# A block's evaluation moved by one pair, the end of the last quarter in an order by hand, and roots refined in three operations

## The chip, the cores and the metric

The kernel runs on one core of a Trainium2 chip. The time is that of the device, in microseconds (us), for one execution; given are the median of several runs and their range. The core has a tensor engine (PE, with its weight loads PEld), a vector engine (DVE), an activation engine (ACT), GpSimd (POOL) and an engine that mostly issues transfers (SP). Each works through its own queue in order and waits on semaphores. Transfers between HBM and the on-chip memory (SBUF) run on 16 DMA engines. Products are accumulated in PSUM, in eight banks of 128 x 512 fp32.

## What is computed

One encoder block over a sequence of 1024 tokens of width 1024, in fp32:

```python
h = h + 0.5 * swiglu(rms_norm(h, ffn1_norm), w_gate, w_up, w_down)      # width 2816
u = rms_norm(h, mix_norm)
z = u @ w_in                     # q, k, v, state-space input, two gates
y_attn = neighbourhood_attention(q, k, v, na_rpb) @ w_attn_out
y_ssm  = s5_branch(s_in, lam, log_dt, b, c, d, glu) @ w_ssm_out   # 32 groups, 2 directions
h = h + (sigmoid(g_attn) * y_attn + sigmoid(g_ssm) * y_ssm) @ w_out
h = h + 0.5 * swiglu(rms_norm(h, ffn2_norm), w_gate2, w_up2, w_down2)
h = h + (p @ ple_w_proj) * sigmoid(rms_norm(h, ple_norm) @ ple_w_gate)
out = rms_norm(h, final_norm)
```

`rms_norm(x, g)` is `x * rsqrt(mean(x*x) + eps) * g`.

## The kernel before

**Layout.** Everything is kept transposed: channels on the 128 partitions, tokens along a row, in two halves t = 0, 1 of 512 tokens. `h[j][t]` is channel block j (of 8), half t.

**Products.** A fp32 operand is split into two parts in the format fp32r: a high part (ACT, L149) and the rest (DVE subtracts, L150). `mm3` (L180 to L182) makes a product from three matmuls of such parts. After each `mm3` the code calls `tick`, which lets one side generator go on when its count has run down: so DVE, ACT and PE work of another stage is placed between the products. `yield n` in a generator means: n ticks until its next piece.

**The feed-forward layers (class `Ffn`).** A 2 x 2 block product is made with seven products in place of eight. The 22 blocks of the hidden width form 11 pairs. Pair 0 of the first layer is special (`run_plain`): its four blocks c = 11, 12, 22, 21 are made as plain fp32 products of h times the norm's gain, without the norm's root r, and DVE multiplies the results by r afterwards (`evac_plain`, L558 to L562). For the second operand of a block (`up`) this is put off: `finish_plain` (L669) does it inside the next block, and for the last block, 21, in pair 1 (L718). There it is six DVE operations: L561, L562 and the four of `combine` (L533, L535, L537, L539), with stores to `a_d`.

Pairs 1 to 10 are items ("A", p, i, g): pair p, product i of seven, g = 0 gate or 1 up, so 14 items for each pair. For each item n the code first prepares the operand of item n + 4 (`prep`, `b_operand`: for i = 2, 3, 5, 6 a subtraction, L425 or L427, then the split), runs four `mm3` into bank Z, X or Y (`ACC7 = "ZXYXYXX"`) and evaluates the result (`evac_a`: a copy on ACT, or L580 and L586 on DVE and the SiLU on ACT). A bank X that takes i = 6 on top of i = 5 must first have been read by L580 for i = 5.

**Who sets the order.** PE's order is the order of the program text for the whole kernel. For DVE and ACT it is so only from the start until `begun`, which was called at item (2,0,0), that is p = 2, i = 0, g = 0 (L720). Afterwards a planner orders DVE, ACT, POOL and SP by a priority (earlier in the text is first, and work under `high_priority` counts as 300 instructions earlier) and by a simulated time. `begun` also closes the pool `up`, which holds r and sums of squares of the start (`acc`, `rs`, `q`), and opens the pool "g" of the state-space parameters in the same room.

**State-space parameters (`gen_all`, L983).** When "g" is there, `gen_params` computes the discretised parameters: some hundred small DVE operations over 46 ticks, ending in the powers `pw` (L818 to L856). POOL copies them to `pe` and `pg` (L867, L870: 68 copies). Then for each of 16 pairs of groups `gen_pair` makes the matrices `gm` and `em` on POOL (L903 to L924); 25 ticks later PE transposes `gm` (`tp`, L947) and multiplies `em` (`kp`, L958). Between `gen_params` and the first `gen_pair` stands `yield 10` (L990).

**Roots (`rstd`, L200).** ACT takes an approximate 1/sqrt, and DVE refines it with one Newton step in four operations (L202 to L205). It is called eleven times. The rows named `gains` hold five norms' gains for each channel; every use of a root is multiplied by one of them.

**The end.** The last layer works in parts: part 0 is half 0, part 1 and 2 are the quarters of half 1 (256 tokens each), part 3 is both quarters at once. `embed(m, part)` (L1582) makes the gate product `pg` and the embedding product `pp` of block m, then sigmoid on ACT (L1596), product and sum on DVE (L1601, L1602), the square for the final norm (`fin[i].add`, L217 to L224), and multiplies h by the final gain on ACT (L1607). `finish(part)` (L1609) takes the root and multiplies four times two blocks by it (L1617), each followed by a store (L1618). The sigmoid and the root need different ACT tables, each loaded by an ACT_TABLE_LOAD; a tiny root on `dummy` (L1600) loads the last one ahead of need. The last steps are blocks 6 and 7 of quarter 1, then of quarter 2; quarter 1 is finished while quarter 2 is made.

Of the kernel before, what the change touches and what calls it, by code (L numbers as in the profile page):

```python
# [11 lines left out]
AF = mybir.ActivationFunctionType  # L12
ALU = mybir.AluOpType
# [3 lines left out]
P = 128  # L17
# [3 lines left out]
NK = 8  # L21
# [17 lines left out]
def encoder_block(ctx, tc, I, out):  # L39
    nc = tc.nc  # L40
    V, A, G, T = nc.vector, nc.scalar, nc.gpsimd, nc.tensor

    sb = ctx.enter_context(tc.tile_pool(name="sb", bufs=1))
    ps = ctx.enter_context(tc.tile_pool(name="ps", bufs=8, space=PSUM))
    dr = ctx.enter_context(tc.tile_pool(name="dr", bufs=1, space=DRAM))

    def const(name, shape, cols=16):


        n = math.prod(shape[1:])  # L50
        t = sb.tile([shape[0], -(-n // cols) * cols], F32, name=name)[:, 0:n]
        if len(shape) == 2:
            return t
        dims = " ".join("abcd"[:len(shape) - 1])
        return t.rearrange(f"p ({dims}) -> p {dims}", **dict(zip("bcd", shape[2:])))
# [12 lines left out]
    def at(kind, shape, dt, name):  # L68
        pool, tag, bufs = cur[kind]
        return pool.tile(list(shape), dt, tag=tag, bufs=bufs, name=name)  # L70
# [10 lines left out]
    def tmp(name, shape=(P, HT), dt=F32):  # L81
        return at("tmp", shape, dt, name)
# [4 lines left out]
    def bank(name):  # L87
        return ps.tile([P, HT], F32, tag="ps", name=name)
# [4 lines left out]

    gains = const("gains", [P, 5, NK])
    nc.sync.dma_start(gains, I["gains"])
    ones = const("ones", [P, P])
    V.memset(ones, 1.0 / SEQ)
    eps = const("eps", [P, 2])
    dummy = eps[:, 1:2]
    eps = eps[:, 0:1]  # L100
# [21 lines left out]
    def start(gen):  # L122
        side["gen"], side["wait"] = gen, next(gen, None)
        if side["wait"] is None:
            side["gen"] = None
# [15 lines left out]
    def drain():  # L141
        gen, side["gen"] = side["gen"], None
        if gen is not None:
            for _ in gen:
                pass
# [6 lines left out]
    def ksl(k):  # L152
        return slice(k * P, (k + 1) * P)
# [35 lines left out]
    def new_h():  # L189
        hb = whole["hb"] = tl("h", 1, [P, 2 * XR], F32, "hbuf")  # L190
        whole["h"] = hb[:, 0:2 * NK * HT].rearrange("p (j t c) -> p j t c", t=2, c=HT)
        return [[hb[:, (2 * j + t) * HT:(2 * j + t + 1) * HT] for t in range(2)] for j in range(NK)]
# [7 lines left out]
    def rstd(m, r, q):  # L200
        A.activation(r, m, AF.Abs_reciprocal_sqrt, bias=eps)
        V.tensor_tensor(q, r, r, ALU.mult)  # L202
        V.scalar_tensor_tensor(q, m, eps, q, ALU.add, ALU.mult)
        V.tensor_scalar(q, q, -0.5, 1.5, ALU.mult, ALU.add)
        V.tensor_tensor(r, r, q, ALU.mult)  # L205

    class Norm:

# [93 lines left out]
    def after(n, fn):  # L302
        def gen():
            yield n
            fn()
        return gen()
# [128 lines left out]
    class Ffn:  # L435
# [261 lines left out]
        def run(self):  # L697
            items = [("C", c, g) for c in C4 for g in range(2)]
            items += [("A", p, i, g) for p in range(1, NP2) for i in range(7) for g in range(2)]
            items += [("B", i, j) for i in range(7) for j in range(NP2)]  # L700
            nl = np_ = 0
            for n, item in enumerate(items):
                while nl < min(len(items), n + self.lb + 1):
                    self.load(items[nl])
                    nl += 1
                while np_ < min(len(items), n + self.la + 1 if n > 7 or not self.seven.plain else 8):
                    if items[np_] not in self.made:
                        self.prep(items[np_])
                    np_ += 1
                if item[0] == "C" and self.seven.plain:  # L710
                    if item[2] == 0:
                        self.run_plain(item[1])
                    self.second = n == 7
                    continue
                if item[0] == "C":
                    self.run_c(*item[1:])
                    continue
                if item == ("A", 1, 3, 0):  # L718
                    self.finish_plain()
                if item == ("A", 2, 0, 0) and self.seven.plain:  # L720
                    self.begun()
                if item[0] == "A":
                    self.run_a(item)
                    continue
                _, i, j = item
                if item in self.hooks:
                    self.hooks[item]()
                if i < 6 or j < NP2 - 4:
                    for q in range(4):
                        self.run_b(i, j, q)  # L730
                elif j == NP2 - 1:
                    for q in range(4):
                        for jj in range(NP2 - 4, NP2):
                            self.run_b(i, jj, q)
                if i == 4 and j == NP2 - 1:
                    self.t0_done()
# [149 lines left out]
    def load_bc(pr):  # L886
        if pr < NPAIR:
            bcs[pr] = pools["g"].tile([P, 6, 2, 16], F32, tag="bc", bufs=1, name="bc")
            nc.sync.dma_start(bcs[pr], I["ssm_bc"][pr])
# [86 lines left out]
    h = new_h()  # L976
# [8 lines left out]
    def gen_all():  # L985
        while "g" not in pools:
            yield 1
        yield from gen_params()
        load_bc(0)
        yield 10  # L990
        for pr in range(NPAIR):
            fin = gen_pair(pr)
            yield 25
            fin()
            yield 4
# [386 lines left out]
    for tt in range(NK):  # L1382
        o = bank("v")
        t, c0 = tt // 4, (tt % 4) * P
# [47 lines left out]
    for hp in range(4):  # L1432
# [3 lines left out]
        n = 2 if hp < 3 else 6  # L1436
# [23 lines left out]
    h = new_h()  # L1460
# [48 lines left out]
    for m0 in range(0, NK, 2):  # L1509
        W, Wn, last = Wn, [], m0 == NK - 2  # L1510
# [34 lines left out]
    def ple_w(*ms):  # L1545
        for m in ms:
            W[m] = loadh(I["wpg"][m])
# [31 lines left out]

    fin = [Fin(i) for i in range(3)]  # L1580

    def embed(m, part):  # L1582
        t, c0, c1 = parts[part] if part < 3 else (1, 0, HT)
        n = c1 - c0
        end = part == 2 and m == NK - 1
        a, b = bank("pg")[:, 0:n], bank("pp")[:, 0:n]
        for k in range(NK):
            mm3(a, W[m][k], [x[:, c0:c1] for x in pn[t][k]], k == 0, k == NK - 1)
            tick()
        for k in range(2):  # L1590
            mm3(b, wpp[m // 4][(m % 4) * 2 + k], [x[:, c0:c1] for x in phl[k, t]], k == 0, k == 1)
            tick()
        s = tmp("ps", [P, n])
        hm = h[m][t][:, c0:c1]
        with tc.high_priority(offset=PRI):
            sg = A.activation(s, a, AF.Sigmoid)  # L1596
            if end:

                with tc.issue_after(sg.ins):
                    dm = A.activation(dummy, eps, AF.Abs_reciprocal_sqrt)  # L1600
            V.tensor_tensor(s, s, b, ALU.mult)  # L1601
            V.tensor_tensor(hm, hm, s, ALU.add)  # L1602
            for i in ((1, 2) if part == 3 else (part,)):
                with (tc.issue_after(dm.ins) if end else nullcontext()):
                    fin[i].add(m, V, end)
        if not end:
            A.activation(hm, hm, AF.Copy, scale=gains[:, 4, m:m + 1])  # L1607

    def finish(part):  # L1609
        f = fin[part]  # L1610
        t, c0, c1 = parts[part]
        f.stat()
        hv = whole["h"][:, :, t, c0:c1]
        if part == 2:
            A.activation(hv[:, NK - 1], hv[:, NK - 1], AF.Copy, scale=gains[:, 4, NK - 1:NK])
        for j in range(0, NK, 2):
            V.tensor_tensor(hv[:, j:j + 2], hv[:, j:j + 2], f.r.unsqueeze(1).broadcast_to([P, 2, f.n]), ALU.mult)  # L1617
            nc.sync.dma_start(out.rearrange("(j p) c -> p j c", p=P)[:, j:j + 2, f.osl], hv[:, j:j + 2])  # L1618

    steps = [(m, 0) for m in range(4)] + [(m, 3) for m in range(4)] + [(m, 0) for m in range(4, NK)]  # L1620
    steps += [(4, 3), (5, 3), (6, 1), (7, 1), (6, 2), (7, 2)]
    ahead = {0: (2,), 1: (3,), 3: (4,), 5: (5,), 6: (6,), 7: (7,)}
    for n, (m, part) in enumerate(steps):
        ple_w(*ahead.get(n, ()))
        if n == 0:
            for k in range(2):
                st = tmp("pst")
                nc.sync.dma_start(st, I["pT"][ksl(k), hsl(1)])
                phl[k, 1] = (tx("pph"), tx("ppl"))
                split(*phl[k, 1], st)  # L1630
            wpp.append(loadh(I["wpp"][1], w_kind="hid"))
        embed(m, part)
        if (m, part) == (3, 0):
            drain()
        if m == NK - 1 and part < 2:
            start(after((14, 9)[part], lambda part=part: finish(part)))
    drain()
    finish(2)


def _layout(x, p, ffn1_norm, ffn1_w_gate, ffn1_w_up, ffn1_w_down, mix_norm, w_in, na_rpb,
# [87 lines left out]
```

## Time and profile before

| | us |
|---|---|
| median of 3 runs | 2150.05 |
| range of the runs | 2149.36 to 2153.09 |
| the profiled execution | 2153.29 |
| its span, first to last instruction | 2151.5 |
| mean granted clock of PE in it | 0.991 |

The profiled execution is 3.2 us above the median; its span leaves out 1.8 us that lie around the instructions. In the profile's tables a row of the timeline reads: start, duration, engine, line, operation, output<-input, shapes, count, and in brackets the idle time before it and what ended it. A row of waits reads: who waited for whom, total us, number of times, the longest. A row of windows reads: the stretch, its length, the busy time of PE, PEld, DVE, ACT and POOL with instruction counts, the granted clock of PE (1 is full), the share of the DMA engines and GB/s. A row of groups reads: shape and count, busy us and mean ns, then idle time before and what ended it.

### The profile page before, as it was taken

To read this page: it belongs to the slowest core of one execution; us is meant where nothing else is said; L and a number is where in the kernel's file an instruction comes from. 1 tells how busy PE (TensorE), PEld (TensorE's weight loads), DVE (VectorE), ACT (ScalarE), POOL (GpSimd) and SP (SyncE) were. 2 spreads that over 40 slices of the span, in tenths; PEclk is the share of its full clock that TensorE was granted. 3 is DMA by queue.
4 is the path that set the end of the run, shared out by engine and by line. 5 is a ranking of instruction groups with operands and counts; after the bars stand their busy time and mean duration, and the time that the engine had idled before them with its cause. 6 is when DMAs were issued, how large, how long until landed. Compare 5 with 4: busy or idle time off the path is not lost.

```text
span 2151.5 us, 28464 instructions
## 1 busy us (share of the span) xinstructions
PE 2101.7 (98%) x9708; PEld 1721.1 (80%) x9708; DVE 1423.6 (66%) x2462; ACT 985.3 (46%) x1830; POOL 392.4 (18%) x680
## 2 busy tenths in 40 slices
PE   8999999999999999999999999899999999999997
PEld 3688888878888888888887788688888888888886
DVE  7886776666967334767744665986666565785845
ACT  6433333334445334666864422543333334545543
POOL 0047555540000008887000000000000000000000
PEclk9999999999999999999999999899999999999999
DMA  3524443466533452223576631242323338533302
GB/s 130 159 86 156 128 131 129 137 208 221 184 116 118 139 176 80 76 68 100 150 216 234 206 103 59 93 156 80 125 89 105 116 94 283 172 107 94 118 20 78
DMA packets 201105, 282.06 MB, mean 131 GB/s; under 512 B 42624, under 2 KB 85760, under 8 KB 200960
## 3 DMA queue, kind: packets, MB, share of 16 engines
q1 hardware_dynamic: 186112, 259.27, 38.1%
q10 hardware_dynamic: 14848, 20.98, 2.8%
q8 instruction: 76, 1.25, 0.2%
q14 instruction: 69, 0.57, 0.1%
HBM read 197.86 MB, written 82.31 MB: 130 GB/s over the span
## 4 chain that ended last, share of the span: by engine, by line
PE 88%; DVE 4%; DMA 4%; ACT 2%; issue 1%; SPq 0%; DVEq 0%; ACTq 0%
PE dx L180 4%; PE dx L181 4%; PE dx L182 4%; PE gx L180 3%; PE gx L182 3%; PE gx L181 3%; PE ux L180 3%; PE ux L182 3%; PE ux L181 3%; PE dy L182 2%; PE dy L181 2%; PE dy L180 2%; PE gy L180 2%; PE uy L180 2%; PE gy L181 2%; PE uy L181 2%
## 5 line engine op out<-in xcount | busy, mean ns | idle before, releaser
L149 ACT CAST wh<-hbuf 128x512 fp32r<-128x512 f32 x280 | 173.3, 622 | 411.3 <-PE gx L181 89.1
L150 DVE TENSOR_TENSOR wl<-hbuf,wh 128x512 fp32r<-128x512 f32 x280 | 208.9, 747 | 133.6 <-ACT wh L149 133.2
L149 ACT CAST wh<-wblk 128x512 fp32r<-128x512 f32 x162 | 100.6, 622 | 165.0 <-PE dx L181 68.5
L150 DVE TENSOR_TENSOR wl<-wblk,wh 128x512 fp32r<-128x512 f32 x162 | 112.4, 695 | 47.3 <-ACT wh L149 43.1
L150 DVE TENSOR_TENSOR al<-araw,ah 128x512 fp32r<-128x512 f32 x154 | 106.9, 697 | 55.0 <-PE dx L181 21.1
L180 PE MATMUL dx<-ah,wh 128*128 128x512 f32 x352 | 138.1, 392 | 0.5 <-DVE hbuf L693 0.5
L182 PE MATMUL dx<-ah,wl 128*128 128x512 f32 x352 | 137.0, 389 | 0.0
L181 PE MATMUL dx<-al,wh 128*128 128x512 f32 x352 | 137.0, 389 | 0.0
L1095 POOL TENSOR_TENSOR sc<-X,rho 128x128 f32<-128x128 f32 x128 | 71.7, 560 | 345.5 <-ACT X L1078 335.5
L180 PE MATMUL gx<-xh,wh 128*128 128x512 f32 x320 | 126.5, 395 | 7.0 <-DVE c L580 7.0
L182 PE MATMUL gx<-xh,wl 128*128 128x512 f32 x320 | 126.0, 394 | 0.0
L181 PE MATMUL gx<-xl,wh 128*128 128x512 f32 x320 | 125.6, 393 | 0.0
L180 PE MATMUL ux<-xh,wh 128*128 128x512 f32 x320 | 124.9, 390 | 0.0
L182 PE MATMUL ux<-xh,wl 128*128 128x512 f32 x320 | 124.5, 389 | 0.0
L181 PE MATMUL ux<-xl,wh 128*128 128x512 f32 x320 | 124.5, 389 | 0.0
L149 ACT CAST ah<-araw 128x512 fp32r<-128x512 f32 x154 | 94.9, 619 | 50.5 <-DVE al L150 13.9
L180 PE MATMUL gt<-xh,wh 128*128 128x512 f32 x256 | 102.9, 402 | 0.0
L182 PE MATMUL gt<-xh,wl 128*128 128x512 f32 x256 | 100.0, 391 | 0.0
L181 PE MATMUL gt<-xl,wh 128*128 128x512 f32 x256 | 99.9, 390 | 0.0
L425 DVE TENSOR_TENSOR hbuf<-hbuf 128x512 f32<-128x512 f32 x120 | 91.1, 759 | 2.4 <-DMA hbuf<-in_wg 0.4
L180 PEld LDWEIGHTS dx<-ah,wh 128*128 128x128 f32 x352 | 66.1, 188 | 15.8 <-DVE hbuf L693 1.7
L180 PEld LDWEIGHTS gx<-xh,wh 128*128 128x128 f32 x320 | 60.9, 190 | 21.1 <-issue 5.5
(375 smaller groups left out, 5769.2 us busy)
## 6 DMA issues: line engine op xcount, KB each, us to landing
araw<-a_d SPq DMA_DIRECT2D x154, 256.0 KB
a_d<-c SPq DMA_DIRECT2D x148, 256.0 KB
wblk<-in_wd SPq DMA_DIRECT2D x88, 256.0 KB
hbuf<-in_wg SPq DMA_DIRECT2D x40, 512.0 KB
hbuf<-in_wu SPq DMA_DIRECT2D x40, 512.0 KB
wst<-in_win SPq DMA_DIRECT2D x26, 512.0 KB
hbuf<-in_xT SPq DMA_DIRECT2D x32, 256.0 KB
h_d<-hbuf ACTq DMA_DIRECT2D x32, 256.0 KB
```

The source lines that it names most:

```text
L149: A.copy(hi, src)
L150: return eng.tensor_tensor(lo, src, hi.bitcast(F32), ALU.subtract)
L180: T.matmul(o, lhsT=wh, rhs=xh, start=first, stop=False, skip_group_check=more)
L181: T.matmul(o, lhsT=wh, rhs=xl, start=False, stop=False, skip_group_check=more)
L182: T.matmul(o, lhsT=wl, rhs=xh, start=False, stop=last, skip_group_check=more)
L425: V.tensor_tensor(b11, (b12, b22, None, None, b21)[i - 2], b11, ALU.subtract)
L1095: G.tensor_tensor(sc, both, rho4, ALU.mult)
```

## The change

Three edits:

1. `finish_plain` for block 21 of pair 0, and `begun` with it, are called at item (2,1,0), so in the third pair's second product. Before, `finish_plain` was called at (1,3,0) and `begun` at (2,0,0). DVE's and ACT's order by hand goes on until there. `yield 10` ahead of the first `gen_pair` becomes `yield 2`.
2. `rstd` gives -2 times the root, in three DVE operations; all `gains` are multiplied by -0.5 once at the start.
3. The end of the last two steps is written out in a function `end`, under an order by hand of DVE and ACT: quarter 1's four scalings are set one behind the sum of block 6, one behind its squares' sum, and two behind the sum of block 7.

```diff
     nc.sync.dma_start(gains, I["gains"])
+
+    V.tensor_scalar(gains, gains, -0.5, None, ALU.mult)
...
         V.tensor_tensor(q, r, r, ALU.mult)
         V.scalar_tensor_tensor(q, m, eps, q, ALU.add, ALU.mult)
-        V.tensor_scalar(q, q, -0.5, 1.5, ALU.mult, ALU.add)
-        V.tensor_tensor(r, r, q, ALU.mult)
+        V.scalar_tensor_tensor(r, q, -3.0, r, ALU.add, ALU.mult)
...
-                if item == ("A", 1, 3, 0):
+                if item == ("A", 2, 1, 0) and self.seven.plain:
                     self.finish_plain()
-                if item == ("A", 2, 0, 0) and self.seven.plain:
                     self.begun()
...
         yield from gen_params()
         load_bc(0)
-        yield 10
+        yield 2
...
+    def first_out():
+        fin[0].stat()
+        finish(0)
+
+    def end():
+
+        start(after(9, fin[1].stat))
+        six = products(6, 2)
+        drain()
+        A.activation(six[2], six[0], AF.Sigmoid)
+        added(*six)
+        finish(1, (0,))
+        fin[2].add(6)
+        scaled(6, six[3])
+        finish(1, (2,))
+        a, b, s, hm = products(7, 2)
+        A.activation(s, a, AF.Sigmoid)
+
+        A.activation(dummy, eps, AF.Abs_reciprocal_sqrt)
+        added(a, b, s, hm)
+        fin[2].add(7, last=True)
+        scaled(7, hm)
+        finish(1, (4, 6))
+        fin[2].stat()
+        finish(2)
...
-    steps += [(4, 3), (5, 3), (6, 1), (7, 1), (6, 2), (7, 2)]
+    steps += [(4, 3), (5, 3), (6, 1), (7, 1)]
...
-        if m == NK - 1 and part < 2:
-            start(after((14, 9)[part], lambda part=part: finish(part)))
+        if m == NK - 1 and part == 0:
+            start(after(14, first_out))
     drain()
-    finish(2)
+    with tc.manual_schedule(engines={mybir.EngineType.DVE, mybir.EngineType.Activation}):
+        end()
```

`products` makes the two products of a block as `embed` did, `added` is L1601 and L1602, `scaled` is L1607, and `finish(part, js)` now scales and stores only the blocks js and leaves the root to its caller.

More of the change, by code (lines that the diff above doesn't have):

```diff
@@ L1580, in encoder_block, with products @@
     fin = [Fin(i) for i in range(3)]
-    def embed(m, part):
+    def products(m, part):
         t, c0, c1 = parts[part] if part < 3 else (1, 0, HT)
         n = c1 - c0
-        end = part == 2 and m == NK - 1
         a, b = bank("pg")[:, 0:n], bank("pp")[:, 0:n]
@@ L1592, in embed @@
             tick()
-        s = tmp("ps", [P, n])
-        hm = h[m][t][:, c0:c1]
-        with tc.high_priority(offset=PRI):
[L1596 to L1602, printed above, removed]
-            for i in ((1, 2) if part == 3 else (part,)):
-                with (tc.issue_after(dm.ins) if end else nullcontext()):
-                    fin[i].add(m, V, end)
@@ L1606, in embed, with added, scaled @@
-        if not end:
-            A.activation(hm, hm, AF.Copy, scale=gains[:, 4, m:m + 1])
-    def finish(part):
+        return a, b, tmp("ps", [P, n]), h[m][t][:, c0:c1]
+    def added(a, b, s, hm):
+        V.tensor_tensor(s, s, b, ALU.mult)
+        V.tensor_tensor(hm, hm, s, ALU.add)
+    def scaled(m, hm):
+        A.activation(hm, hm, AF.Copy, scale=gains[:, 4, m:m + 1])
+    def embed(m, part):
+        a, b, s, hm = products(m, part)
+        with tc.high_priority(offset=PRI):
+            A.activation(s, a, AF.Sigmoid)
+            added(a, b, s, hm)
+            for i in ((1, 2) if part == 3 else (part,)):
+                fin[i].add(m)
+        scaled(m, hm)
@@ L1610, in finish @@
+    def finish(part, js=range(0, NK, 2)):
         f = fin[part]
         t, c0, c1 = parts[part]
-        f.stat()
         hv = whole["h"][:, :, t, c0:c1]
-        if part == 2:
-            A.activation(hv[:, NK - 1], hv[:, NK - 1], AF.Copy, scale=gains[:, 4, NK - 1:NK])
-        for j in range(0, NK, 2):
+        for j in js:
             V.tensor_tensor(hv[:, j:j + 2], hv[:, j:j + 2], f.r.unsqueeze(1).broadcast_to([P, 2, f.n]), ALU.mult)
             nc.sync.dma_start(out.rearrange("(j p) c -> p j c", p=P)[:, j:j + 2, f.osl], hv[:, j:j + 2])
+    def first_out():
+        fin[0].stat()
+        finish(0)
@@ new lines, in end @@
+    def end():
[9 more added lines that the diff above has]
+        a, b, s, hm = products(7, 2)
+        A.activation(s, a, AF.Sigmoid)
+        A.activation(dummy, eps, AF.Abs_reciprocal_sqrt)
+        added(a, b, s, hm)
+        fin[2].add(7, last=True)
[3 more added lines that the diff above has]
+        finish(2)
```

## The prediction

> **What bounds the kernel now.** I read the page first, then the list of waits of PE over the whole run, then the timelines of PE, DVE, ACT and POOL around each wait that the edits touch, and last the end of the run.
>
> ```profile
> PE 2101.7 (98%) x9708; PEld 1721.1 (80%) x9708; DVE 1423.6 (66%) x2462; ACT 985.3 (46%) x1830; POOL 392.4 (18%) x680
> PE gx L180 <- DVE c L580: 7.0, 2, 4.5
> PE ms L242 <- ACT sq L217: 2.9, 1, 2.9
> ```
>
> PE is busy for 2101.7 of 2151.5 us, so the change can only win from the remaining 49.8 us, and from matmuls that run at a lower clock behind a gap. PE's order is written out by hand and no matmul is added or dropped: the question is which gaps go and which come. Both waits above are touched: the one of 4.5 us under "gx <- c" (two waits, 7.0 in all), and the one at the end (ms L242).
>
> **Part 1: the first pair's last block.** The gap of 4.5 us lies at the end of pair 1:
>
> ```profile
> 97.69 0.39 PE L182 MATMUL ux<-xh,wl 128*128 128x512 f32 x1
> 102.58 0.47 PE L180 MATMUL gx<-xh,wh 128*128 128x512 f32 x1 [4.51 <-DVE c L580]
> 107.00 0.39 PE L180 MATMUL ux<-xh,wh 128*128 128x512 f32 x1
> 109.73 0.39 PE L180 MATMUL gz<-xh,wh 128*128 128x512 f32 x1
> 104.00:106.00 2.00, 2.00 (x6) 1.60 (x5) 1.97 (x4) 0.13 (x1) 0.00 (x0) 0.50 0.21 81
> ...
> 30.00:64.00 34.00, 34.00 (x81) 15.09 (x80) 32.31 (x54) 17.56 (x29) 0.00 (x0) 1.00 0.24 76
> 88.39 0.69 DVE L150 TENSOR_TENSOR wl<-hbuf,wh 128x512 fp32r<-128x512 f32 x1 [0.74 <-ACT wh L149]
> 89.00 0.68 DVE L561 TENSOR_TENSOR c<-u,c 128x512 f32<-128x512 f32 x1
> 89.72 0.69 DVE L562 TENSOR_TENSOR c<-c,rs 128x512 f32<-128x512 f32 x1
> 93.12 0.68 DVE L427 TENSOR_TENSOR hbuf<-hbuf 128x512 f32<-128x512 f32 x1
> 101.75 0.69 DVE L580 TENSOR_TENSOR c<-gx,c 128x512 f32<-128x512 f32 x1
> ```
>
> PE's last matmul before the gap takes its slot of 0.23 us and is through at 97.92; the next starts at 102.58, so the gap is 4.66. The 12 matmuls behind it take 4.42 (102.58 to 107.00), the next 12 take 2.73 (107.00 to 109.73): 1.69 more, at the granted clock of 0.50 in the row of 104 to 106 (seventh figure). The stall costs 6.35 us in all. It ends with L580 at 101.75, which stands in DVE's queue behind everything from 89.00 on, the six operations of `finish_plain` (L561 to L539, 89.00 to 93.12 = 4.12 us) among them. Without these the same chain starts at 89.00 and L580 at 97.63; PE starts 0.83 behind it (102.58 less 101.75), at 98.46, 0.54 late. DVE is also two shorter roots earlier here (part 2, 0.41 each, at 20 and 38 us), as its queue has few holes on the way (32.3 of 34 us busy from 30 to 64): 97.64, so PE does not stop. **PE gains 6.35 us at this place.**
>
> What is moved is not free. `finish_plain` now stands in the hand-written DVE order behind the last operand of (2,3,0), and the pools opened after it wait for its L562, the last reader of the pool `up`:
>
> ```profile
> POOL bd L937 <- DVE c L562: 90.1, 1, 90.1
> 90.48 0.34 SPq L775 DMA_DIRECT2D g_prm<-in_ssm_p  x1
> 93.72 0.18 DVE L756 TENSOR_SCALAR g_prm<-g_prm 128x32 f32<-128x32 f32 x1
> 109.93 0.69 DVE L586 TENSOR_TENSOR c<-ux,c 128x512 f32<-128x512 f32 x1
> 142.40 0.28 DVE L856 TENSOR_TENSOR pw<-pw,tq 128x128 f32<-128x128 f32 x1
> 109.70:142.70 33.00, 33.00 (x147) 27.31 (x146) 30.14 (x115) 13.43 (x25) 8.18 (x36) 1.00 0.36 112
> ...
> 143.40 0.56 POOL L867 COPY g_pe<-pw 128x16 f32<-128x16 f32 x1
> 154.64 1.05 POOL L922 TENSOR_TENSOR gm<-g_pg,bb 128x512 f32<-128x512 f32 x1
> 161.54 1.88 POOL L924 TENSOR_TENSOR em<-em,tg 128x576 f32<-128x576 f32 x1
> 165.50 0.60 PE L947 MATMUL tp<-ident,gm 128*128 128x128 f32 x4
> ```
>
> POOL waited until 90.54 for L562 and SP sent the state-space parameters at 90.48, right behind it. DVE's parameter chain (`gen_params`) ran in what the operands left, in a stretch where DVE is busy 30.1 of 33 us; it ended at 142.68. POOL then copied the last powers (143.4 to 154.6) and made `gm` and `em`, `em` at 163.42. PE reads `gm` at 165.50 and `em` 0.53 later, at 166.03. So `em` has 2.6 us to spare, and with PE 6.35 us earlier (159.68) it is 3.7 us too late even if POOL and DVE did all at the same time as before. `yield 10` becoming 2 keeps these matmuls at their place in PE's order (eight ticks later start, eight ticks fewer), so they meet POOL's chain earlier, not later.
>
> When does `em` come? L586 of (1,6,1) moves with PE, to 103.6. Four operations of `combine` follow (0.72 each, the pace of `finish_plain`'s 89.00 to 89.72): 107 with the start. Three operands, subtraction, ACT's copy and subtraction, at 0.69 + 0.74 idle + 0.60 = 2.0 us each (the row of 88.39): 112.5. `finish_plain`: 116.6, L562 ending at 113.9. Parameters asked for then are used some 3 us later (90.48 to 93.72), at 117. From there to the last power DVE has, in order of emission, 11 splits and 5 subtractions at 0.60 (9.6), six L580 and three L586 at 0.65 (5.9), and the parameter operations themselves. For these I take what is left in the old stretch 106.1 to 142.7:
>
> ```profile
> L150 DVE TENSOR_TENSOR wl<-hbuf,wh 128x512 fp32r<-128x512 f32 x15 | 10.3, 689 | 2.9 <-ACT wh L149 2.9
> L425 DVE TENSOR_TENSOR hbuf<-hbuf 128x512 f32<-128x512 f32 x7 | 4.8, 688 | 0.0
> L867 POOL COPY g_pe<-pw 128x16 f32<-128x16 f32 x16 | 8.1, 520 | 0.1
> L867 POOL COPY g_pe<-pw x36: 204/275/682, 91.3 to 154.0; 128x16 f32<-128x16 f32 x36
> ```
>
> Its 15 splits, 9 subtractions (two of them L427) and 13 operations on results (six L580, three L586, four of `combine`), at 0.60, make 22.2, idle time some 4, so the parameters took about 10.3. Sum: 117 + 9.6 + 5.9 + 10.3 + 2 idle = 144.8, say 144.5; `em` 20.7 later (163.42 less 142.68), at 165.2. PE, at 159.68, waits until 165.3: 5.6 us, and 1.7 us go to the lower clock as behind the other gap. Against 166.03 before: 165.3 + 1.7 - 166.0 = **+1.0 us for the whole of part 1**. Both ends: were the parameters ahead of all splits and subtractions, they would be done by 135, `em` by 156, and the whole gain of 6.35 stands. Were they done at 149 and the 28 copies of the last powers (16 of L867, 12 of L870) as slow as 0.60 us each, `em` would come at 175 and the stage lose 11. I take the middle, as the same count of the old stretch gives its end within a microsecond.
>
> The longest copy took 0.68 us and the shortest 0.20, the same form: POOL is slower while DVE runs. [...]
>
> **Part 2: roots in three operations.** L204 goes and L205 takes its work:
>
> ```profile
> L204 DVE TENSOR_SCALAR q<-q x2: 428/428/429, 20.4 to 37.7; 128x512 f32<-128x512 f32 x2
> 1359.39 0.75 DVE L203 SCALAR_TENSOR_TENSOR rq<-ms,eps,rq 128x512 f32<-128x512 f32 x1
> 1360.66 0.42 DVE L204 TENSOR_SCALAR rq<-rq 128x512 f32<-128x512 f32 x1
> 1385.62 2.07 PE L240 MATMUL ms<-acc,ones 128*128 128x512 f32 x2 [5.59 <-DVE acc L224]
> 2144.45 0.29 DVE L204 TENSOR_SCALAR rq<-rq 128x256 f32<-128x256 f32 x1
> 4.00 1.28 ACT L345 ACT_TABLE_LOAD   x1 [4.00 <-DMA hbuf<-in_xT]
> ```
>
> One operation with its start, 0.47 (0.33 for 256 columns) goes; the new L205 is of L203's kind, 0.06 longer. So 0.41 for each of eleven roots, 0.27 at the end. Only where DVE's queue reaches PE does it count: at 1385.62, whose wait ends with a queue that runs without a hole from 1359 on; there it is 0.33 less 0.06, **-0.3 us**. The other roots lie beside PE, at nothing; were PE to wait on one, 0.41. The new scaling of `gains` at the start waits for a transfer that SP sends just ahead of the first block of x; ACT's first work waits for that block until 4.00. Hidden: nothing, and at most 0.3 us.
>
> **Part 3: the end.**
>
> ```profile
> 2132.35 1.28 ACT L201 ACT_TABLE_LOAD   x1
> 2137.92 2.49 DVE L1617 TENSOR_TENSOR hbuf<-hbuf,rs 128x512 f32<-128x512 f32 x4
> 2140.33 0.42 DVE L1601 TENSOR_TENSOR ps<-ps,pp 128x256 f32<-128x256 f32 x1
> 2139.58 0.20 ACT L1600 ACTIVATE eps<-eps 128x1 f32<-128x1 f32 x1
> 2141.24 0.42 ACT L217 ACTIVATE sq<-hbuf 128x256 f32<-128x256 f32 x1 [1.45 <-DVE hbuf L1602]
> 2145.24 2.50 DVE L1617 TENSOR_TENSOR hbuf<-hbuf,rs 128x512 f32<-128x512 f32 x4
> ```
>
> The last block's L1601 stands at 2140.33 behind four scalings of the quarter before (from 2137.92, 0.60 each). By hand, two of them go behind it, and of the other two one falls into the hole while ACT squares block 6. All of it comes 0.67 earlier by two roots (0.41 of `first_out`, which delays quarter 1 through DVE's queue, and 0.27 of quarter 1). So L1601 comes 1.2 to 1.8 and 0.67 earlier, at 2137.9 to 2138.5, and its sum is done 0.9 later (0.45 each), by 2138.8 to 2139.4. The square then waits for ACT: the dummy, done at 2139.78, is done at 2139.1. So the square starts at 2139.1 in place of 2141.24, 2.1 earlier. Then PE, ACT and DVE as before, less 0.27 for the root, and perhaps 0.5 from PE's clock: L1617 at 2142.5 for 2145.24, **-2.7 us**, bounds -1.5 and -3.3. The lower end is for a sum that is late, the upper for both roots and the clock in full. The transfers of the last scalings go out behind them as before.
>
> **Sum.** +1.0 - 0.3 - 2.7 = -2.0 us. The profiled execution took 2153.29 (span 2151.5), so 2151.3 for one like it; the median of the runs is 3.2 lower, 2150.05, and I set the sum against that: **2148.0 us**.
>
> **The rivals.**
> *The parameters come in time.* If DVE's planned order puts them ahead of the operands, or POOL copies at 0.20, PE does not stop at the transposes: -6.35 - 0.3 - 2.7 = -9.3, 2140.7; partly so, -5 to -9. For it: DVE has holes of 0.74 behind each ACT copy. Against: none before L562, at 113.9.
> *The planner moves another wait.* DVE and ACT outside the hand-written parts are planned anew. The second "gx <- c" (7.0 in all less 4.5) behind the last pair's products costs 2.5 and some 1.7 of clock: gone, the total is -6.2, 2143.9; a second like it, +2.2, 2152.2.
> *POOL's chain is later than the lead and the end can pay for* (slower). The place is the same, `em` before PE's first products. It decides from `em` at 171.6 on: 7.4 us later than the break-even of 164.2 less what parts 2 and 3 give (3.0) makes +4.4. At 175 it is +7.8, 2157.9. It needs DVE's last power at 149 and copies near their longest time; for it, that DVE's lead over PE has gone by then.
> *The edit changes nothing at its place:* then the 4.5 us gap stays; the row of L561 in the queue ahead of L580 excludes it.
>
> The Trainium skill ("TensorE: Matmul & The Clock Gate", What's actually happening) gives half rate after an idle window of about 3.4 us, free-running. By that, the new wait of 5.6 would be charged like the old one. The trace shows the half clock behind 4.51 us idle.
>
> **How the numbers follow.** Late products, total within 4.3 us of zero: 0.44, own range 2146 to 2154. In time: 0.30. Planner takes the other wait away: 0.10; adds one: 0.04. Slower chain: 0.12. A difference of 0.2% (4.3 us) is about what a measurement of this kernel tells from none; so faster 0.40, same 0.48, slower 0.12. The range reaches from the case in time to a chain at about 172: 2140.8 to 2154.5.
>
> **What would show it.** Right: no PE gap ahead of pair 1's last product gx (i = 6); L561 and L562 on DVE at about 112 to 114; the first POOL operation at about 114; PE waiting some 5 us at the first `tp` and `kp`, half clock behind; the last square on ACT right behind the dummy. Wrong: a PE gap at gx again, now behind a split; no wait at `tp` (rival one); new gaps between 170 and 2100.

## The result: 0.17% slower

| | before | after |
|---|---|---|
| median | 2150.79 us (18 runs) | 2155.51 us (18 runs) |
| range | 2146.61 to 2159.84 | 2152.39 to 2159.21 |
| ratio, 95% interval | | 1.0017 [1.0009, 1.0025] |
| span of the profiled execution | 2151.5 | 2152.4 |

The forecast was 2148.0 us, a gain of 2.0. The ratio says a loss of 3.7 us (0.0017 of 2151), between 1.9 and 5.4. Line numbers behind the changed places are one or two higher than before (L149 is now L151, L580 is L581, L562 is L563), from L1582 on they differ more.

**The profile after.** First the totals of the page, then rows of the list of waits of PE, the longest first.

```profile
PE 2102.2 (98%) x9708; PEld 1722.5 (80%) x9708; DVE 1418.0 (66%) x2452; ACT 983.4 (46%) x1830; POOL 386.7 (18%) x680
```

```profile
PE tp L947 <- POOL gm L924: 7.2, 1, 7.2
...
PE gx L182 <- DVE c L581: 4.4, 2, 2.5
...
PE ms L243 <- ACT sq L218: 1.4, 1, 1.4
```

PE's sum of busy time tells nothing (2102.2 for 2101.7). The list does: the 4.5 us under "gx <- c" are gone, the wait at the end (ms L243) has halved, and at the head stands a wait that before did not have, 7.2 us at the first transposes. The timelines of PE, DVE, SP and POOL show how it comes:

```profile
98.06 0.39 PE L184 MATMUL ux<-xh,wl 128*128 128x512 f32 x1
98.35 0.47 PE L182 MATMUL gx<-xh,wh 128*128 128x512 f32 x1
...
160.38 0.50 PE L182 MATMUL gx<-xh,wh 128*128 128x512 f32 x1 [1.92 <-DVE c L581]
169.27 1.12 PE L947 MATMUL tp<-ident,gm 128*128 128x128 f32 x4 [7.24 <-POOL gm L924]
170.63 1.92 PE L958 MATMUL kp<-em,bd 128*32 128x128 f32 x8 [0.24 <-POOL em L924]
...
116.97 0.69 DVE L563 TENSOR_TENSOR c<-c,rs 128x512 f32<-128x512 f32 x1
117.73 0.33 SPq L775 DMA_DIRECT2D g_prm<-in_ssm_p  x1
117.78 0.21 POOL L937 MEMSET bd<- 128x128 f32 x1 [117.33 <-DVE c L563]
120.67 0.15 DVE L756 TENSOR_SCALAR g_prm<-g_prm 128x32 f32<-128x32 f32 x1
155.96 0.28 DVE L856 TENSOR_TENSOR pw<-pw,tq 128x128 f32<-128x128 f32 x1
169.17 1.40 POOL L924 TENSOR_TENSOR em<-em,tg 128x576 f32<-128x576 f32 x1
```

`gx` at 98.35 follows the product ahead of it without a stop; the half clock behind it is gone too. Below: the last reader of the pool `up` at 116.97, the parameters asked for right behind it, used from 120.67 on, the last power done at 156.24 (142.68 before), `em` at 170.57 (163.42 before). PE is at the transposes at 162.03 and stands until 169.27. The windows show the clock behind that wait (the seventh figure), half until past 174:

```profile
169.00:171.00 2.00, 1.49 (x6) 1.06 (x7) 0.00 (x0) 0.58 (x2) 2.00 (x4) 0.50 0.17 48
171.00:174.00 3.00, 3.00 (x12) 2.15 (x11) 0.95 (x2) 0.47 (x3) 3.00 (x7) 0.50 0.43 131
174.00:176.00 2.00, 2.00 (x7) 1.58 (x6) 0.69 (x2) 0.99 (x2) 1.80 (x4) 0.61 0.22 49
176.00:178.00 2.00, 2.00 (x11) 1.65 (x10) 0.48 (x1) 0.11 (x1) 1.98 (x2) 1.00 0.13 29
```

So the second pair of groups' `kp` starts at 194.28, 6.88 later than before (187.40). At the end of the run (timelines of ACT and DVE):

```profile
2135.96 1.28 ACT L203 ACT_TABLE_LOAD   x1
2142.91 0.20 ACT L1636 ACTIVATE eps<-eps 128x1 f32<-128x1 f32 x1
2143.02 0.40 ACT L218 ACTIVATE sq<-hbuf 128x256 f32<-128x256 f32 x1
...
2141.80 0.41 DVE L1595 TENSOR_TENSOR ps<-ps,pp 128x256 f32<-128x256 f32 x1
2146.16 2.50 DVE L1615 TENSOR_TENSOR hbuf<-hbuf,rs 128x512 f32<-128x512 f32 x4
```

The last square stands right behind the tiny root on `dummy`. From the first table load of quarter 1 to the last scalings it takes 10.20 us (2135.96 to 2146.16), 12.89 before (2132.35 to 2145.24).

### The profile page after: what moved, and what is told of

The parts are those of the page before. It is cut to its first block, busy times and chain, and to the rows that moved or that the text cites. A ratio compares the mean times of both kernels' runs of the same rounds, so it can differ in the third digit from the quotient of the medians.

```text
span 2152.4 us, 28451 instructions
## 1 busy us (share of the span) xinstructions
PE 2102.2 (98%) x9708; PEld 1722.5 (80%) x9708; DVE 1418.0 (66%) x2452; ACT 983.4 (46%) x1830; POOL 386.7 (18%) x680
## 4 chain that ended last, share of the span: by engine, by line
PE 87%; DVE 4%; DMA 3%; ACT 3%; issue 1%; POOL 1%; SPq 1%; DVEq 0%; ACTq 0%
PE dx L182 4%; PE dx L183 4%; PE dx L184 4%; PE gx L182 3%; PE ux L182 3%; PE gx L184 3%; PE gx L183 3%; PE ux L183 3%; PE ux L184 3%; PE dy L182 2%; PE dy L184 2%; PE dy L183 2%; PE gt L182 2%; PE gt L183 2%; PE gt L184 2%; PE gy L182 2%
## 5 line engine op out<-in xcount | busy, mean ns | idle before, releaser
L151 ACT CAST wh<-hbuf 128x512 fp32r<-128x512 f32 x280 | 173.5, 622 | 421.2 <-PE gx L183 87.0
L151 ACT CAST wh<-wblk 128x512 fp32r<-128x512 f32 x162 | 100.4, 622 | 167.0 <-PE dx L183 67.9
L151 ACT CAST ah<-araw 128x512 fp32r<-128x512 f32 x154 | 95.0, 619 | 48.4 <-PE dx L183 12.6
L183 PEld LDWEIGHTS dx<-al,wh 128*128 128x128 f32 x352 | 66.1, 188 | 14.1 <-issue 0.5
```

The source lines that it names most:

```text
L151: A.copy(hi, src)
L183: T.matmul(o, lhsT=wh, rhs=xl, start=False, stop=False, skip_group_check=more)
```

## The experiments

Two theories stood at the start. A: edit 1 costs what its products wait for the parameters, and edits 2 and 3 give 3 to 4 us back. B: the loss comes from the new plan of DVE and ACT elsewhere. Each kernel was timed beside runs of the kernel before on the same chip; "-x us" is the ratio's distance from 1 times 2151.

| kernel | ratio to before, 95% interval | us |
|---|---|---|
| after | 1.0017 [1.0009, 1.0025] | +3.7 |
| e1: without edit 1 | 0.9980 [0.9969, 0.9990] | -4.3 |
| e2: edit 1 alone | 1.0022 [1.0012, 1.0032] | +4.7 |
| e3: first products 18 ticks later | 0.9967 [0.9955, 0.9979] | -7.1 |
| e4: edit 1 by half | 0.9995 [0.9984, 1.0006] | -1.1 |
| e5: edit 2 alone | 0.9982 [0.9971, 0.9993] | -3.9 |
| e6: edit 3 alone | 0.9988 [0.9979, 0.9997] | -2.6 |
| e8: e3, pairs one tick closer | 0.9976 [0.9966, 0.9987] | -5.2 |
| e9: after, with fewer parameter operations | 0.9985 [0.9975, 0.9995] | -3.2 |
| e10: e3, one transfer moved to SP | 0.9953 [0.9940, 0.9967] | -10.1 |
| e11: e1, the same | 0.9983 [0.9973, 0.9992] | -3.7 |
| e12: e3, that transfer moved to POOL | 0.9964 [0.9951, 0.9976] | -7.7 |

### e1 and e2: the change in two parts

e1 puts edit 1 back as it was; e2 is edit 1 alone:

```diff
-                if item == ("A", 2, 1, 0) and self.seven.plain:
+                if item == ("A", 1, 3, 0):
                     self.finish_plain()
+                if item == ("A", 2, 0, 0) and self.seven.plain:
                     self.begun()
...
-        yield 2
+        yield 10
```

> Edits 2 and 3 without edit 1 (finish_plain at (1,3,0), begun at (2,0,0), yield 10). Theory A, the loss of the change lies wholly in what edit 1 does to the parameter chain: the gap of 4.5 us at pair 1's last gx is back, the first tp does not wait, and the kernel is 3 to 4 us faster than before (the end 3.2, as the traces of before and after differ between 2030 and the end, and some tenths from the roots). Theory B, the loss comes from a new plan of the stages behind 200 us, which the shorter roots bring about: the same or slower than before.

> Edit 1 alone. Theory A: PE waits some 7 us at the first tp as in the changed kernel, the second pair's kp lies at 194 in place of 187.5, and the whole is 5 to 7 us slower than before. Theory B: within 2 us of before, as the stage gains at gx what it loses at tp, and the plan behind it is the old one.

PE's timeline, of e1:

```profile
102.61 0.77 PE L182 MATMUL gx<-xh,wh 128*128 128x512 f32 x1 [4.00 <-DVE c L581]
...
166.28 0.60 PE L948 MATMUL tp<-ident,gm 128*128 128x128 f32 x4
```

and of e2:

```profile
98.36 0.47 PE L180 MATMUL gx<-xh,wh 128*128 128x512 f32 x1 [0.44 <-DVE c L580]
...
169.29 1.11 PE L946 MATMUL tp<-ident,gm 128*128 128x128 f32 x4 [6.40 <-POOL gm L923]
```

Edit 1 takes the first gap and makes the second; without it the first is back and there is no second. The two parts sum to +0.4 for +3.7 measured, within the intervals (2.2 us each way for each part). Theory A holds as to where the loss sits; that it is the wait, e3 shows below. Of B nothing is needed.

### e5 and e6: what roots and end are worth apart

e5 has edit 2 alone, e6 edit 3 alone.

> Edit 2 alone on the kernel before (roots in three operations, gains scaled at the start). Theory (my term): one operation of 0.47 us less in each of eleven roots, which counts only where DVE's queue reaches PE (the br wait near 1385): -0.3 us, the time within 1 us of the kernel before, gap at pair 1's last gx still 4.0 to 4.6. Rival: the end's two roots and the shifted queue are worth more: -1.5 to -2.5, most of what edits 2 and 3 gave together (3.3).

> Edit 3 alone on the kernel before (order of the last quarter's end by hand, old four-operation roots). Theory: it gives most of the 3.3 us that edits 2 and 3 gave together: -2.3 to -3, the last square right behind the dummy. Rival: half of the gain at the end is from the two shorter roots: -1 to -1.5.

Single executions do not rank such kernels: between the second `kp` and the norm at about 1977, where the edits change next to nothing, the profiled executions of before, e1, e2, e5, e6 and after took 1786.7 to 1793.3 us. Stages tell more. From the traces (starts of `ms` at about 1977 and about 2029, and the span):

| | before | e5 | e6 | e1 | e2 | after |
|---|---|---|---|---|---|---|
| second `kp` | 187.40 | 186.47 | 187.15 | 188.19 | 193.87 | 194.28 |
| `ms` to `ms`, 1977 to 2029 | 52.31 | 51.80 | 52.34 | 51.81 | 52.32 | 51.82 |
| from there to the end | 121.6 | 120.1 | 119.3 | 118.5 | 121.6 | 118.5 |

The kernels with three-operation roots are 0.5 shorter in the second row. Matmul by matmul, before and after part at one place only, of which before's row of PE's timeline is:

```profile
1995.73 0.50 PE L180 MATMUL dx<-ah,wh 128*128 128x512 f32 x1 [0.23 <-DVE hbuf L693]
```

DVE's L693, which adds the products of the old layer to h, stands behind the root in DVE's queue. With the old roots PE stops for it twice (0.28 at 1994.53, and the row), with the new ones once. The end: roots alone -1.5, order alone -2.3, both -3.1, so they share 0.7. Together the roots and the order give 3.6 us, which e1 bears out (3.3 by its medians, 4.3 by its ratio). In e5 my term of -0.3 for the roots missed (its rival, 1.5 to 2.5, is nearer: 0.5 + 1.5 = 2.0 by the stages); in e6 the theory held.

### e3: the same products, 18 ticks later

```diff
         yield from gen_params()
         load_bc(0)
-        yield 2
+        yield 20
```

> The changed kernel with yield 20 in place of 2 ahead of the first gen_pair, so PE meets the first tp 18 ticks (12.2 us) later in its own order. Theory A: em at 170.6 is then in time for PE at about 172, the wait of 7.2 us and the half clock behind it go, and the kernel is 8 to 10 us faster than before (6.3 at gx, 3 to 4 at the roots and the end). Theory B: within 2 us of the changed kernel.

```profile
171.22 0.60 PE L947 MATMUL tp<-ident,gm 128*128 128x128 f32 x4
171.75 1.06 PE L958 MATMUL kp<-em,bd 128*32 128x128 f32 x8
...
482.44 0.50 PE L183 MATMUL dz<-al,wh 128*128 128x512 f32 x1 [2.68 <-DVE al L152]
491.69 0.50 PE L182 MATMUL dz<-ah,wh 128*128 128x512 f32 x1 [1.00 <-ACT ah L151]
```

PE's timeline of e3 shows no wait at `tp` and `kp`, so edit 1 now keeps its gain. With one number changed the whole change is 7.1 us faster than before. The interval reaches from 4.5 to 9.7, so the expected 8 to 10 are neither shown nor excluded. The lower rows show what may be short of them: the later pairs now end among the down products, where two waits of 2.7 and 1.0 come instead of the second "gx <- c".

### e4: the reader of `up` earlier, the pools as before

```diff
-                if item == ("A", 2, 1, 0) and self.seven.plain:
+                if item == ("A", 1, 6, 0):
                     self.finish_plain()
+                if item == ("A", 2, 0, 0) and self.seven.plain:
                     self.begun()
...
-        yield 2
+        yield 10
```

> The changed kernel with finish_plain at (1,6,0), behind the evaluation that PE waits for but two items ahead of begun, which is back at (2,0,0) with yield 10. Theory A: no gap at gx, L562's counterpart at about 103 and not 117, the last power by about 146, em at about 164; PE waits 3 to 5 us at tp, and the kernel is 2 to 6 us faster than before. Theory B: like the changed kernel, within 2 us.

DVE's and PE's timelines:

```profile
102.86 0.69 DVE L563 TENSOR_TENSOR c<-c,rs 128x512 f32<-128x512 f32 x1
152.28 0.28 DVE L857 TENSOR_TENSOR pw<-pw,tq 128x128 f32<-128x128 f32 x1
...
167.28 1.11 PE L948 MATMUL tp<-ident,gm 128*128 128x128 f32 x4 [7.28 <-POOL gm L925]
```

A miss, and the one that told most. The last reader of `up` comes 14.1 us earlier than in after (102.86 for 116.97), and the last power only 3.7 (152.56 for 156.24). So the time at which the parameters are let in does not set their end by itself; it takes the longer, the earlier they start: 47 us here (105.30, where the first parameter operation starts, to 152.56), 35.6 in after, 49 in before (93.72 to 142.68). In these stretches DVE's timelines have 57, 35 and 50 operations of 128x512.

### e9: a shorter chain

What is left between is DVE itself. e9 leaves the second exponential out of the parameters (17 operations by its text, where the expectation counted 22, and the six ticks of its `yield`s), so that its powers are not those of the reference.

```diff
         xr, y = c32("xr"), c32("y")
...
-        s, q = yield from exp_parts(xr, "e")
```

> The whole change, with the second exponential of the parameters left out (22 small operations on DVE; the powers are then those of the first exponential). Theory: the first wait at tp is set by the length of the parameter chain on DVE, where each few small operations have a large operation of the operands put between them: the chain takes 28 us in place of 35.6, last power at 148 to 149.5, em at 163 to 167, the wait at tp 0 to 3.5 in place of 7.2, the time 3 to 6 us below the kernel after. Rival: the chain's start (L563 at 117) and POOL's copies set it: em not before 169, wait over 5, time within 2 us of the kernel after.

DVE's, POOL's and PE's timelines of e9:

```profile
149.29 0.28 DVE L856 TENSOR_TENSOR pw<-pw,tq 128x128 f32<-128x128 f32 x1
162.38 1.40 POOL L924 TENSOR_TENSOR em<-em,tg 128x576 f32<-128x576 f32 x1
162.47 1.11 PE L947 MATMUL tp<-ident,gm 128*128 128x128 f32 x4 [7.25 <-POOL gm L924]
```

The last power comes 6.7 us earlier than in after, and `em` 6.8 earlier, as the theory said. The rival's claim that start and copies set `em` falls. The 17 operations are worth 2.2 us of DVE at the mean of 0.13 (11.9 us for 92, counted below); the rest of the 6.7 goes with the large operations that no longer stand between them (28 of 128x512 in place of 35, 4.2 us at 0.60), but for 0.5 by which the chain starts earlier. The wait itself did not shrink (7.25), against the theory and as the rival had it: with six ticks fewer (0.68 each, 4.1 us) and with 0.2 in place of the wait of 1.92 at `gx` that after has on the way, PE came to the transposes at 155.22 in place of 162.03. By the ratios the time is 6.9 us better than after's, so e9 shows what sets `em`, not what the wait costs.

### e8, e10, e11 and e12: what the later pairs run into

e8 is e3 with 28 in place of 29 ticks for each pair of groups. e10, e11 and e12 take the transfer of `fm` out of ACT's queue, as in e10:

```diff
-        nc.scalar.dma_start(f_d[pr], fm)
+        nc.sync.dma_start(f_d[pr], fm)
```

> The whole change, with the first pair's products 18 ticks later (as in e3_products_later) and the sixteen pairs one tick closer together (28 in place of 29), so that the last pair ends about where it did in the kernel after. Theory: the two dz waits (2.7 and 1.0 us plus 0.3 each, at 482 to 492 in e3) came from the late last pairs alone, and go: no wait at tp or kp, ms landmark at about 640, time 3 to 5 below e3_products_later, so 8.5 to 10 below the kernel before (ratio 0.9955). Rival: the closer pairs make POOL late for each pair (a pair's POOL work against 28 ticks of PE), tp waits appear at the later pairs, and the time is at that of e3 or above (-6 or less).

> As e3_products_later (whole change, first pair's products 18 ticks later), with the transfer of fm to f_d (L953) issued by SP in place of ACT. In e3, before, after and e1 the last pair's L953 stands in ACT's queue for 2 to 5 us behind an earlier weight transfer, and the casts behind it come late: gx waits 0.6 to 2.5, or dz 2.7 and 1.0. Theory: with the issue out of ACT's queue these waits and their half clock go: the last pair's kp follows the one before by 21.4 to 22 us in place of 26.6, no wait over 0.5 at 440 to 500; the time 4 to 5 below e3_products_later, 9 to 11 below the kernel before (ratio 0.9950 to 0.9958). Rival: SP's queue is held in its place and the blocks it sends come late, new waits between 180 and 500, time at that of e3 or above.

> As e1_no_move (edits 2 and 3 alone), with L953's transfer issued by SP in place of ACT. Theory: the second gx wait (1.07 in e1's trace, 2.46 in before's) goes with its half clock, the first (4.0) stays: 1 to 4 below e1, 5 to 7 below the kernel before. Rival: SP's queue is held, time at that of e1 or above.

> As e10, with L953's transfer issued by POOL (whose transfers wait for fewer earlier ones). Theory: as e10, 9 to 11 below the kernel before. Rival: POOL, held for ACT's copy of fm in each pair, makes the next pair's gm and em late: tp waits at the later pairs, time above e3.

What led there: in this stretch before and e6 have the same instructions, and "gx <- c" took 2.46 us in the one and 0.65 in the other. ACT's timeline, of before and then of e6:

```profile
470.96 0.33 ACTq L953 DMA_DIRECT2D f_d<-fm  x1
471.54 0.26 ACT L962 COPY ka<-kp 32x128 f32<-32x128 f32 x1 [4.87 <-DMA wblk<-in_wd]
```

```profile
468.73 0.33 ACTq L953 DMA_DIRECT2D f_d<-fm  x1
469.30 0.26 ACT L962 COPY ka<-kp 32x128 f32<-32x128 f32 x1 [2.89 <-DMA wblk<-in_wd]
```

`fm` is written by 466.2 in both, but its transfer is issued 2.2 us later in the one than in the other, behind a transfer of weights, and the casts behind it in ACT's queue come as much later. That the issue alone is to blame, fell with e11: there it was gone from ACT's queue, `gx` still waited 1.36 us at 473.21, and the gain over e1 did not come. e8 missed too: no `dz` wait is left in it and none came at `tp`, but there are waits of 1.52 (`gx`, 468.66) and 2.25 (`ux`, 473.95). The windows of before suggest why a single queue is not the cause (the eighth figure is the share of the DMA engines):

```profile
458.00:462.00 4.00, 4.00 (x19) 3.30 (x19) 1.65 (x2) 1.10 (x2) 2.87 (x6) 1.00 0.29 71
466.00:470.00 4.00, 4.00 (x21) 3.19 (x19) 4.00 (x3) 0.66 (x2) 4.00 (x5) 1.00 0.98 341
470.00:474.00 4.00, 2.11 (x10) 1.42 (x8) 2.20 (x5) 1.44 (x4) 3.16 (x4) 1.00 1.01 334
474.00:478.00 4.00, 3.42 (x9) 2.72 (x10) 3.02 (x5) 1.14 (x2) 0.00 (x0) 0.64 0.93 345
```

From 466 to 478 the DMA engines are full at about 340 GB/s, with DVE and POOL busy for the whole of 466 to 470 besides. In e10, whose time came as expected, one wait of 1.76 is left, and the last `kp` follows the one before by 23.4 us (21.4 to 22 expected, 26.6 in e3). e10 has the lowest ratio here, 0.9953 of before; that it is faster than e3 is likely and not shown, as their intervals meet, and e12, with the same idea, is where e3 is. Which transfer ends last in this stretch stays open.

## Why the prediction was wrong

**Part 1, the gap (right).** PE does not stop at `gx`, with 98.35 against 98.46; in e2, with the old roots, 0.44 of the forecast 0.54 is left. The 12 matmuls from there on are through at 107.00 in before and at 101.17 in after, 5.8 earlier for the 6.35 forecast.

**Part 1, the parameters (wrong, and the step that failed).** The mechanism was as said: `em` late behind POOL, POOL behind DVE's powers, these behind the moved last reader of `up`. The size was not. The prediction had the last power at 144.5 (144.8 by its sum) and `em` at 165.2; they came at 156.24 and 170.57. The step is the sum "117 + 9.6 + 5.9 + 10.3 + 2 idle". Its terms by DVE's windows and groups in after:

```profile
120.60:156.25 35.65, 35.65 (x159) 29.50 (x158) 33.23 (x128) 12.40 (x23) 11.91 (x33) 1.00 0.42 143
```

```profile
L152 DVE TENSOR_TENSOR wl<-hbuf,wh 128x512 fp32r<-128x512 f32 x13 | 9.0, 692 | 1.5 <-ACT wh L151 1.5
L426 DVE TENSOR_TENSOR hbuf<-hbuf 128x512 f32<-128x512 f32 x6 | 4.1, 688 | 0.0
L428 DVE TENSOR_TENSOR hbuf<-hbuf 128x512 f32<-128x512 f32 x2 | 1.4, 687 | 0.0
```

- *The start*: 117 in the sum, 120.67 in the trace, 3.7 later, since L563 came at 116.97 in place of about 113.2. The prediction had `finish_plain` in the order by hand; but work that the text has behind `begun` (L581 at 112.76 and 115.77 among it) came ahead of it and in between.
- *The large operations*: 25 in the sum (11 splits, 5 subtractions, 9 results), 35 in the trace: 13, 8 and, by the timeline, 14, four of them `combine` of the third pair and three that of `finish_plain`, which the sum had done by then. Ten more at 0.60 are 6.0.
- *The small ones*: 10.3 in the sum, 11.9 in the trace (92 operations).

That is 3.7 + 6.0 + 1.6 = 11.3 of the 11.7. The wrong idea was "in order of emission": that DVE does what the text has ahead of the last power and nothing else. The parameters are a chain in which nearly each operation needs the one before, and the planner puts a large operation of the next pair between. So their length follows what else is ready, as e4 (47 us) and e9 bear out. A kernel that gives the parameters a higher priority was not run.

**POOL's copies (wrong, the other way).** Last power to `em` was carried over as 20.7; it took 14.3. Of the 6.4, 4.5 lie ahead of the first operation on `gm` (7.45 us behind the last power, 11.96 before) and 1.9 in the six operations on `gm` and `em` (6.9 us for 8.8). The rows of groups in the copies' stretch (143 to 170) of after:

```profile
L867 POOL COPY g_pe<-pw 128x16 f32<-128x16 f32 x32 | 8.1, 258 | 20.1 <-DVE pw L818 19.8 <-DVE pw L853 0.3
```

A copy took 258 ns in place of 520 in the same stretch of before. DVE was busy for only 3.55 of 14.35 us from 156.25 to 170.60, and for 18.80 of 20.74 behind before's last power: PE's stop had left it without work (it stood idle for 10.86 us until ACT had read PE's `kp`). In before the copies of 0.67 us start some 0.1 us behind a DVE operation on two operands in SBUF (L150, L425, L533), while copies beside L586 on `ux`, which lies in PSUM, took 0.21. So the prediction's "POOL is slower while DVE runs" was right and came out reversed: the stall that was to grow by it made the copies fast. 11.7 less 6.4 is the 5.3 by which `em` missed.

**PE.** The prediction had a wait of 5.6 and 1.7 of clock. Measured: 7.24 and 0.24 of wait, and 1.92 at another `gx` (160.38) that was not foreseen and ends with DVE's L581, in the same crowd. The clock cost 2.9: the second `kp` follows the first by 23.65 in place of 21.37, and the first follows `tp` by 0.6 more beside its wait of 0.24. Part 1 came to +6.9, not +1.0; the terms (-5.8, 1.92, 7.24, 0.24, 2.9) make 6.5, and 0.4 stays unassigned. The slower rival, "POOL's chain is later than the lead and the end can pay for", had the place right, and a last power beyond its 149, but not its slow copies; its own rule, `em` less 164.2, gives +6.4 at the measured `em`.

**Part 2 (too small).** -0.3 was said where the stages show -0.5 at the norm of 1977 to 2029 alone, at a place taken as hidden. At the norm behind 1356 (1356.04 to 1385.62 before, 1361.12 to 1390.49 after) the difference is 0.2, but e2, with the old roots, took 29.23 there, so the -0.3 was not resolved. The root's share at the end, put into part 3 as 0.67, is 1.5 alone and 0.8 on top of edit 3.

**Part 3 (right).** -2.7 with bounds to -3.3; 3.1 measured, roots' share included. The dummy bound the last square, as said.

**The sum.** 6.9 - 0.5 - 3.1 = +3.3, within the interval of the result.

## What to carry to other kernels

Moving work out of one wait is to be priced at the next place where an in-order engine meets a chain that was fed by that work; here a delay of 27 us in the start of a chain with 2.6 us to spare. The length of a chain of small dependent operations on a shared engine isn't its busy time: it is what the scheduler puts between them, so carry over from a trace how many large operations stand between start and end, not those due by text order. If the consumer's place is free to choose, as with `yield` here, set it behind the moved producer first and measure that version: 18 ticks turned +3.7 us into -7.1.

## What the hardware showed besides

**Two streams slow each other.** In before, at the last pair of groups, DVE's and POOL's timelines:

```profile
462.95 0.68 DVE L150 TENSOR_TENSOR wl<-wblk,wh 128x512 fp32r<-128x512 f32 x1
467.08 1.66 DVE L586 TENSOR_TENSOR c<-c,c 128x512 f32<-128x512 f32 x1
468.66 1.54 DVE L150 TENSOR_TENSOR al<-araw,ah 128x512 fp32r<-128x512 f32 x1
466.56 1.62 POOL L922 TENSOR_TENSOR em<-g_pe,bc 128x576 f32<-128x576 f32 x1
```

DVE's operations of 0.68 us take 1.5 to 1.7 beside POOL's large ones, and POOL's first `em` operation 1.62, where after's, at 165.71 with DVE nearly idle, took 1.16. The Trainium skill ("SBUF — State Buffer"), section "SBUF: two separate sides", calls the port pair that the two share an exclusive lock, held by the one that starts first for its whole instruction (on DVE's side by operations with two SBUF inputs, for one). The trace agrees: L586, begun at 467.08, ends at 468.74, 0.56 behind POOL's `em` (468.18), and 0.60 is its slot where nothing holds it. The hold can outlast one instruction, as DVE's timeline of e9 shows:

```profile
156.65 7.68 DVE L536 TENSOR_TENSOR c<-c,c 128x512 f32<-128x512 f32 x1
```

It ends 0.55 us behind the last of POOL's six operations on `gm` and `em`, which ran from 156.89 to 163.78 without a hole. The other way round, POOL's L904, 0.29 us at 170.96 in after, took 3.69 from 149.62 on, beside a row of DVE operations without a hole until 153.15. That nothing else held either of the two is not shown. The prediction reckoned with a loss on POOL's side alone.

**The half clock depends on where the gap falls.** The windows of before and of e3 behind gaps of 2.46 and 2.68 us:

```profile
476.00:478.00 2.00, 2.00 (x6) 1.58 (x5) 1.02 (x2) 0.00 (x0) 0.00 (x0) 0.50 0.86 325
```

```profile
482.00:486.00 4.00, 3.56 (x16) 2.93 (x17) 2.87 (x7) 1.76 (x5) 0.00 (x0) 1.00 1.07 402
```

The shorter gap was charged (0.50), the longer was not (1.00). Gaps of 2.47 in after (481.45) and of 2.46 in e4 (478.98) were charged as well. The Trainium skill ("TensorE: Matmul & The Clock Gate", Part 1: The HAM clock gate) has a free-running window of about 3.4 us, which agrees with a cost that depends on the gap's place; a gap below that length can evidently be charged.
